# Table copies paced through a ScalarE cell, a third accumulator for the output projections, and two sums' buffers

## The chip, the cores and the metric

The kernel runs on one core of one Trainium2 chip. The metric is device time in microseconds (us): the median over runs. TensorE (PE) does matmuls, VectorE (DVE) and ScalarE (ACT) do elementwise work and empty the accumulators, GpSimd (POOL) does some elementwise work and issues a few transfers, SyncE (SP) issues most transfers. Each engine works through its own queue in order.

## What is computed

Two layers of a mixer network over T = 640 tokens (512 latent, 128 context) of width 2048. In float32 throughout, and cut to what matters here:

```python
mod = silu(cond) @ w_ada[l] + b_ada[l]            # 2048 x 6144, two condition vectors
shift, scale, gate = split(mod, 3)
h = rmsnorm(x, norm_g[l]) * (1 + scale) + shift
q, k, v, ag, lx, lg, hv, hx1, hx0, hg = split(h @ w_in[l])      # 2048 x 7168
att = diff_attention(q, k, v) * silu(ag)          # 8 heads
lru = rglru(conv(lx)) * silu(lg)
hy  = conv(hx0) * long_conv(conv(hv) * conv(hx1), hyena_filters) * silu(hg)
x = x + gate * (concat(att, lru, hy) @ w_out[l])  # 2048 x 2048
# after layer 2: y = rmsnorm(x, final_g); also context keys, values and LRU states
```

## The kernel before

**Projections.** Activations lie transposed as 16 chunks of 128 features by 640 tokens, each as a high and a low part (`A`). A weight block of 512 x 128 comes by one transfer (`wr`, line 380; four buffers). ScalarE casts it to `wh` and VectorE subtracts to `wl` (lines 177 and 178; four buffers each). `gemm` (line 418) computes one output chunk `m` from four such blocks, 24 matmuls of 320 columns each, into an accumulator `g` of two PSUM banks. The pool `pm` has two of these. Of the other four banks, two are the one buffer of `psS` (line 161), and two are the two buffers of `psT`, one bank each (line 164). The loads of a block are given a priority 600 places ahead of where they stand in the program. The framework makes each engine's queue from the program order, these priorities and its own planned times; a queue once made is run in order.

**Modulation steps.** `ada_steps` (line 327) is a generator, called `hook`. Each step loads one 128 x 512 piece of `w_ada` (`wa`, line 335) and makes two VectorE accumulations into `adas` (line 341). After 16 steps there is a seventeenth, "the turn": eight transposes into two `psT` (line 348) and two sums out of them (line 349). `adas` has one buffer. `gemm` advances the hook `hr` times per weight block, 1.5 in the output projection of layer 0, so six steps per chunk. Inside that projection (`wap` set) `wa` has four buffers.

**Tables.** After the second of the first three attention gates has been placed, `load_tabs` (line 746) allots the tables of the long convolution, in memory that the attention pool gives back. `tab_steps` (line 758) loads them in ten parts, one per weight block. So that a part is not fetched too early, GpSimd first copies one element of the block's `wh` into the part (line 762), then issues its transfer (line 763). The attention pool's last user is a transfer `rd<-oh` (line 1213). The third gate is the first product whose blocks pace the tables. The filters of the convolution (lines 593 to 640) come next in the program; their inputs are loaded by transfers on ScalarE's queue: `hid` (line 599), `w` (line 606), `drow` (line 622), `dec` (line 624). Line 632 multiplies into a `psT`, line 634 empties it.

**Output projection** (line 470). For chunk `m`, `old(m)` brings the residual. In layer 0 it is loaded as `xt`, transposed into the one `psS` (line 1268) and copied by ScalarE to `xo` (lines 1493 and 1494; two buffers). `new(m)` empties the accumulator with three VectorE instructions (line 1502) that read `xo`, then sums squares (lines 476 to 480). Chunks 0 and 1 are computed together; then `gemm` of chunk m stands ahead of `new(m)` in the program. Chunks 14 and 15 go through `gemm_parts` (line 396) together, in two halves of the tokens; the first three input projections of layer 1 go the same way, the third into `psS`. In layer 1 `turned` (line 1507) scales by `final_g`, transposes back into `psS` (line 1514) and copies to `Y` (lines 1518 and 1520). `stats` (line 461) uses a `psT`.

Of the kernel before, what the change touches and what calls it, by code (L numbers as in the profile page):

```python
# [20 lines left out]
NL = 512  # L21
# [115 lines left out]
class K:  # L137
# [189 lines left out]
    def ada_steps(self, todo):  # L327

        nc = self.nc
        for l, pc in todo:  # L330
            wv = self.i["w_ada"][l].rearrange("(a p) m -> p a m", p=128)
            acc = self.tl(self.sm, [128, 2, 512], tag="adas", bufs=1)
            for k in range(KC):
                w = self.tl(self.wap or self.W, [128, 512], F32, "wa", bufs=4 if self.wap else 2)
                nc.sync.dma_start(w, wv[:, k, pc * 512:(pc + 1) * 512])
                for s in range(2):
                    c = self.cs[:, k, s:s + 1]
                    if k == 0:
                        nc.vector.tensor_scalar(acc[:, s], w, c, None, op0=ALU.mult)
                    else:  # L340
                        nc.vector.scalar_tensor_tensor(acc[:, s], w, c, acc[:, s], op0=ALU.mult, op1=ALU.add)  # L341
                if k == KC - 1:
                    yield
                    sl = slice(pc * 4, pc * 4 + 4)
                    for s in range(2):
                        pt = self.psT()
                        for c in range(4):
                            nc.tensor.transpose(pt[:, c * 128:(c + 1) * 128], acc[:, s, c * 128:(c + 1) * 128], self.ident)
                        nc.vector.reduce_sum(self.par[l]["mod"][:, sl, s], pt.rearrange("p (c k) -> p c k", c=4), axis=AX.X)
                    self.ada_bias(l, pc * 4, 4)  # L350
                yield

    def ada_fin(self, l, c0, n, sb, tag):
# [41 lines left out]

    def gemm_parts(self, wd, ms, rhs, order, parts, keeps):

        nc = self.nc
        ps = [self.pm.tile([128, 2, 512], F32, name=self.nm("g_%d" % m), tag="m") if n < 2 else self.psS() for n, m in enumerate(ms)]
        ws = {}  # L400
# [16 lines left out]

    def gemm(self, wd, ms, rhs, order=range(KC)):

        nc = self.nc  # L420
        ps = [self.pm.tile([128, 2, 512], F32, name=self.nm("g_%d" % m), tag="m") for m in ms]
        for a in range(4):
            ks = order[4 * a:4 * a + 4]
            for m, p in zip(ms, ps):
                with self.tc.high_priority(offset=600):
                    wh, wl = self.load_w(wd, ks[0], m)
                self.last = wh
                if self.hook is not None:
# [317 lines left out]
    def load_tabs(self, pool):  # L746
# [4 lines left out]
        tp = self.tl(pool, [128, 2, 3, 128], F32R, tag="tp")  # L751
        self.tabs = (tb, rw, tp)
        w = 2 * TCE_W
        parts = [(tb[:, a, b, c:c + n], i["dft"][:, a, b, c:c + n]) for a in range(2) for b in range(2) for c, n in ((0, w), (w, 512))]
# [3 lines left out]
    def tab_steps(self, parts):  # L758
        nc = self.nc
        for t, src in parts:  # L760
            c = t if len(t.shape) == 2 else t[:, 0, 0, :]
            nc.gpsimd.tensor_copy(c[:, 0:1], self.last[:, 0, 0:1].bitcast(F32))
            nc.gpsimd.dma_start(t, src)
            yield True
# [705 lines left out]
    def out_proj(self, l):  # L1470
# [13 lines left out]
        def old(m):  # L1484
            xo = self.tl(pool, [128, T], tag="xo", bufs=2)
            if l == 0:
# [3 lines left out]
                nc.sync.dma_start(xt[:, 4, :], self.i["x_prompt"][0, :, c])  # L1490
                ps = self.psS()
                self.turn(lambda b: xt[:, b, :], 0, (ps[:, 0, :], ps[:, 1, :NP]))
                nc.scalar.copy(xo[:, :NL], ps[:, 0, :])
                nc.scalar.copy(xo[:, NL:], ps[:, 1, :NP])
            else:
# [11 lines left out]
        def turned(m, x, lo, hi):  # L1507

            V.tensor_scalar(x[:, lo:hi], x[:, lo:hi], self.par[l]["final_g"][:, m:m + 1], None, op0=ALU.mult)
            ps = self.psS()  # L1510
            b0, b1 = lo // 128, hi // 128
            for b in range(b0, b1):
                dst = ps[:, 0, b * 128:(b + 1) * 128] if b < 4 else ps[:, 1, :128]
                nc.tensor.transpose(dst, x[:, b * 128:(b + 1) * 128], self.ident)  # L1514
            c = slice(m * 128, (m + 1) * 128)
            bs = min(b1, 4)
            if b0 < bs:
                nc.scalar.copy(Y[:, b0:bs, c], ps[:, 0, b0 * 128:bs * 128].rearrange("p (b c) -> p b c", c=128))
            if b1 == 5:
                nc.scalar.copy(Y[:, 4, c], ps[:, 1, :128])  # L1520

# [14 lines left out]
        for m in range(KC - 2):  # L1536
# [3 lines left out]
            elif m > 1:  # L1540
                xos[m] = old(m)
                pq[m] = self.gemm(wd, [m * 128], ms, MIX_ORDER)[0]
            p = pq.pop(m)
# [11 lines left out]
        else:  # L1555
            parts = (0, HT, 0, 0), (HT, T, 1, 0)
        g = self.gemm_parts(wd, [m * 128 for m in zb], ms, MIX_ORDER, parts, [zp] * 8)
        p = dict(zip(zb, next(g)))
# [42 lines left out]
        first = [COL_HX0, COL_HG, COL_HX0 + 128]  # L1601
        g = self.gemm_parts(self.i["w_in"][1], first, hs, range(KC), ((0, HT, 0, 0), (HT, T, 1, 0)), [None] * 4 + [zp] * 8)
        ps = next(g)
# [51 lines left out]
```

## Time and profile before

| | |
|---|---|
| median of 3 runs | 2690.55 us (2690.27 to 2692.62) |
| the profiled execution's own time | 2696.49 us |
| its span, first to last instruction | 2694.7 us |
| mean granted TensorE clock | 0.984 |
| busy: PE, DVE, ACT, POOL | 96%, 71%, 40%, 10% |
| DMA over the span | 354.85 MB, mean 132 GB/s |

Times in rows are us from the span's start. In a timeline row stand start, duration, engine, line, operation, output <- inputs, shapes, how many instructions were merged, and in brackets the idle time of the engine before the first of them and what ended it. `SPq` and `ACTq` are issues of transfers. A granted clock of 1.00 is 2.4 GHz, 0.50 is 1.2 GHz.

### The profile page before, as it was taken

To read this page: it belongs to the slowest core of one execution; us is meant where nothing else is said; L and a number is where in the kernel's file an instruction comes from. 1 tells how busy PE (TensorE), PEld (TensorE's weight loads), DVE (VectorE), ACT (ScalarE), POOL (GpSimd) and SP (SyncE) were. 2 spreads that over 40 slices of the span, in tenths; PEclk is the share of its full clock that TensorE was granted. 3 is DMA by queue.
4 is the path that set the end of the run, shared out by engine and by line. 5 is a ranking of instruction groups with operands and counts; after the bars stand their busy time and mean duration, and the time that the engine had idled before them with its cause. 6 is when DMAs were issued, how large, how long until landed. Compare 5 with 4: busy or idle time off the path is not lost. (4 is left out here: it accounts for less than half of the span.)

```text
span 2694.7 us, 45940 instructions
## 1 busy us (share of the span) xinstructions
PE 2585.5 (96%) x17579; PEld 2491.2 (92%) x17579; DVE 1905.7 (71%) x3503; ACT 1074.9 (40%) x1965; POOL 280.1 (10%) x398
## 2 busy tenths in 40 slices
PE   6999999999999999989999999999999999999998
PEld 3689999999999999979988999999999989999997
DVE  5478779889888676578789467786887656565333
ACT  5224655454544222222234256545455522224222
POOL 2001210000001222100001022000000031120000
PEclk9999999999999999989999999999999999999999
DMA  9864233333333534577664422242332252345333
GB/s 283 295 192 134 80 104 106 101 95 118 97 115 111 170 112 137 163 238 228 206 201 136 126 73 82 87 118 68 104 90 63 59 157 87 112 143 169 91 99 116
DMA packets 442326, 354.85 MB, mean 132 GB/s; under 512 B 26401, under 2 KB 367216, under 8 KB 442106
## 3 DMA queue, kind: packets, MB, share of 16 engines
q1 hardware_dynamic: 428938, 336.39, 41.5%
q10 hardware_dynamic: 9280, 9.33, 1.1%
q0 software_dynamic: 3888, 6.20, 0.8%
q8 instruction: 138, 2.26, 0.4%
q14 instruction: 82, 0.67, 0.1%
HBM read 316.51 MB, written 35.32 MB: 131 GB/s over the span
## 5 line engine op out<-in xcount | busy, mean ns | idle before, releaser
L440 PE MATMUL g<-A,wh 128*128 128x320 f32 x8256 | 1595.3, 312 | 14.5 <-DVE xf L1502 9.4
L440 PEld LDWEIGHTS g<-A,wh 128*128 128x128 f32 x8256 | 1307.9, 189 | 17.8 <-issue 9.7
L440 PE MATMUL g<-A,wl 128*128 128x320 f32 x4128 | 953.8, 310 | 0.0
L177 ACT CAST wh<-wr 128x512 fp32r<-128x512 f32 x584 | 360.4, 619 | 972.3 <-PE g L440 664.3
L440 PEld LDWEIGHTS g<-A,wl 128*128 128x128 f32 x4128 | 695.5, 189 | 0.5 <-DVE wl L178 0.3
L178 DVE TENSOR_TENSOR wl<-wr,wh 128x512 fp32r<-128x512 f32 x584 | 421.5, 726 | 358.3 <-ACT wh L177 346.2
L341 DVE SCALAR_TENSOR_TENSOR adas<-wa,cs,adas 128x512 f32<-128x512 f32 x480 | 349.8, 763 | 31.7 <-DMA wa<-in_w_ada 30.1
L1233 ACT ACTIVATE e<-e,mx 128x768 f32<-128x768 f32 (+1 forms) x160 | 133.7, 836 | 67.0 <-DVE e L1232 66.6
L1232 DVE TENSOR_SCALAR_CACHE_REDUCE e<-pS 128x768 f32<-128x768 f32 (+1 forms) x160 | 131.3, 820 | 9.2 <-ACT e L1233 3.1
L1195 POOL TENSOR_TENSOR oq<-ot 128x640 f32<-128x640 f32 x16 | 20.9, 1303 | 898.0 <-ACT ot L1191 793.1
L732 PE MATMUL pS<-kk,qq 128*128 128x384 f32 (+1 forms) x288 | 100.9, 350 | 6.9 <-DVE e L1232 6.5
L540 PE MATMUL gp<-A,wh 128*128 128x320 f32 x512 | 103.9, 321 | 0.6 <-DVE e L546 0.3
L414 PE MATMUL g<-A,wh 128*128 128x320 f32 (+2 forms) x384 | 93.0, 326 | 10.9 <-ACT A L517 6.2
L540 PEld LDWEIGHTS gp<-A,wh 128*128 128x128 f32 x512 | 80.7, 191 | 18.3 <-issue 6.7
L732 PE MATMUL pS<-kl,qq 128*128 128x384 f32 (+1 forms) x288 | 96.0, 333 | 0.0
L178 DVE TENSOR_TENSOR wtl<-pt,wth 128x512 fp32r<-128x512 f32 (+1 forms) x144 | 70.4, 523 | 25.5 <-ACT wth L177 25.3
L177 ACT CAST wth<-pt 128x512 fp32r<-128x512 f32 (+1 forms) x144 | 59.7, 459 | 66.7 <-PE pt L1176 66.4
L414 PEld LDWEIGHTS g<-A,wh 128*128 128x128 f32 x384 | 67.7, 197 | 14.5 <-ACT A L517 7.2
L1502 DVE SCALAR_TENSOR_TENSOR xf<-g,mod,xo 128x128 f32<-128x128 f32 (+3 forms) x96 | 38.7, 436 | 55.4 <-PE g L440 20.4
L1239 DVE SCALAR_TENSOR_TENSOR e<-e,rz,e 128x768 f32<-128x768 f32 (+1 forms) x80 | 70.7, 883 | 1.7
L732 PEld LDWEIGHTS pS<-kk,qq 128*128 128x128 f32 x288 | 54.4, 189 | 17.5 <-DVE e L1232 12.2
L546 DVE TENSOR_TENSOR e<-e,gp 128x640 f32<-128x640 f32 x40 | 32.6, 818 | 41.5 <-PE gp L540 41.3
(376 smaller groups left out, 3258.2 us busy)
## 6 DMA issues: line engine op xcount, KB each, us to landing
wr<-in_w_in SPq DMA_DIRECT2D x448, 256.0 KB
wa<-in_w_ada SPq DMA_DIRECT2D x256, 256.0 KB
wr<-in_w_out SPq DMA_DIRECT2D x128, 256.0 KB
wada<-in_w_ada SPq DMA_DIRECT2D x28, 1024.0 KB
mx<-md SPq DMA_DIRECT2D x28, 320.0 KB
md<-ot SPq DMA_DIRECT2D x16, 320.0 KB
gm<-md SPq DMA_DIRECT2D x16, 320.0 KB
R<-rd SPq DMA_DIRECT2D x16, 320.0 KB
```

What stands on the lines that cost most here:

```text
L177: self.nc.scalar.copy(hi, src)
L178: self.nc.vector.tensor_tensor(lo, src, hi.bitcast(F32), op=ALU.subtract)
L341: nc.vector.scalar_tensor_tensor(acc[:, s], w, c, acc[:, s], op0=ALU.mult, op1=ALU.add)
L414: nc.tensor.matmul(p[:, j, o:o + c1 - c0], lhsT=w[:, c, :], rhs=rhs[k][x][:, c0:c1], start=(a == 0 and c == 0 and n == 0), stop=(a == 3 an ...
L440: nc.tensor.matmul(p[:, j, :HT], lhsT=w[:, c, :], rhs=rhs[k][x][:, j * HT:(j + 1) * HT], start=(a == 0 and c == 0 and n == 0), stop=(a == ...
L540: nc.tensor.matmul(p[:, j, :HT], lhsT=w, rhs=rhs[k0 + c][x][:, j * HT:(j + 1) * HT], start=(c == 0 and t == 0), stop=(c == n - 1 and t == 2))
L546: nc.vector.tensor_tensor(v, v, p[:, :, :HT], op=ALU.add)
L732: self.nc.tensor.matmul(out, lhsT=a, rhs=b, start=(n == 0), stop=(n == len(pairs) - 1))
L1232: V.tensor_scalar(e[:, :nk].rearrange("p (a b) -> p a b", a=nhf), ps[:, :nhf, :hw], -1.0, None, op0=ALU.mult, op1=ALU.min, accum_out=mx)
L1233: nc.scalar.activation(e[:, :nk], e[:, :nk], AF.Exp, scale=-1.0, bias=mx, accum_out=Z[:, c:c + 1])
L1239: V.scalar_tensor_tensor(es[0][:, :nk], es[1][:, :nk], rz[:, 1:2], es[0][:, :nk], op0=ALU.mult, op1=ALU.add)
L1502: V.scalar_tensor_tensor(x[:, a:b], p, mod[:, 32 + m, s:s + 1], xo[:, a:b], op0=ALU.mult, op1=ALU.add)
```

## The change

- The GpSimd copy of a table part reads a cell of a small tile `cells`; ScalarE writes that cell from the block's `wh`, once per weight block while tables are being loaded.
- In both output projections every third chunk (m = 2, 5, 8, 11, 14) accumulates in `psS`. `old` and `turned` use the two `psT` in place of `psS`.
- Inside the output projection of layer 0 `adas` gets two buffers of that pool's own, and the turn of one piece is made at the fourth step of the next. A piece takes 16 steps there, the last one 17.

```diff
     def ada_steps(self, todo):
         nc = self.nc
+        pend = None
         for l, pc in todo:
             wv = self.i["w_ada"][l].rearrange("(a p) m -> p a m", p=128)
-            acc = self.tl(self.sm, [128, 2, 512], tag="adas", bufs=1)
+            acc = self.tl(self.wap, [128, 2, 512], tag="adas", bufs=2) if self.wap else self.tl(self.sm, [128, 2, 512], tag="adas", bufs=1)
             for k in range(KC):
...
-                if k == KC - 1:
-                    yield
-                    sl = slice(pc * 4, pc * 4 + 4)
-                    for s in range(2):
...
-                    self.ada_bias(l, pc * 4, 4)
+                if k == 3 and pend is not None:
+                    self.ada_turn(*pend)
+                    pend = None
                 yield
+            pend = l, pc, acc
+            if not self.wap or (l, pc) == todo[-1]:
+                self.ada_turn(*pend)
+                pend = None
+                yield
+
+    def ada_turn(self, l, pc, acc):
+        nc = self.nc
+        for s in range(2):
+            pt = self.psT()
+            for c in range(4):
+                nc.tensor.transpose(pt[:, c * 128:(c + 1) * 128], acc[:, s, c * 128:(c + 1) * 128], self.ident)
+            nc.vector.reduce_sum(self.par[l]["mod"][:, pc * 4:pc * 4 + 4, s], pt.rearrange("p (c k) -> p c k", c=4), axis=AX.X)
+        self.ada_bias(l, pc * 4, 4)
 
-    def gemm_parts(self, wd, ms, rhs, order, parts, keeps):
+    def gemm_parts(self, wd, ms, rhs, order, parts, keeps, banks):
-        ps = [self.pm.tile([128, 2, 512], F32, name=self.nm("g_%d" % m), tag="m") if n < 2 else self.psS() for n, m in enumerate(ms)]
+        ps = [self.psS() if s else self.acc(m) for m, s in zip(ms, banks)]
 
-    def gemm(self, wd, ms, rhs, order=range(KC)):
+    def gemm(self, wd, ms, rhs, order=range(KC), third=False):
-        ps = [self.pm.tile([128, 2, 512], F32, name=self.nm("g_%d" % m), tag="m") for m in ms]
+        ps = [self.psS() if third else self.acc(m) for m in ms]
...
                     wh, wl = self.load_w(wd, ks[0], m)
-                self.last = wh
+                if self.tabl is not None:
+                    self.cn += 1
+                    nc.scalar.copy(self.cells[:, self.cn - 1:self.cn], wh[:, 0, 0:1].bitcast(F32))
...
     def load_tabs(self, pool):
+        self.cells, self.cn = self.tl(self.sm, [128, 16], tag="cell", bufs=1), 0
...
     def tab_steps(self, parts):
-            nc.gpsimd.tensor_copy(c[:, 0:1], self.last[:, 0, 0:1].bitcast(F32))
+            nc.gpsimd.tensor_copy(c[:, 0:1], self.cells[:, self.cn - 1:self.cn])
             nc.gpsimd.dma_start(t, src)
...
     def out_proj(self, l):
         def old(m):
-                ps = self.psS()
-                self.turn(lambda b: xt[:, b, :], 0, (ps[:, 0, :], ps[:, 1, :NP]))
-                nc.scalar.copy(xo[:, :NL], ps[:, 0, :])
-                nc.scalar.copy(xo[:, NL:], ps[:, 1, :NP])
+                pt, pp = self.psT(), self.psT()
+                self.turn(lambda b: xt[:, b, :], 0, (pt, pp[:, :NP]))
+                nc.scalar.copy(xo[:, :NL], pt)
+                nc.scalar.copy(xo[:, NL:], pp[:, :NP])
         def turned(m, x, lo, hi):
-            ps = self.psS()
...
+            for u, v in ((b0, min(b1, 4)), (max(b0, 4), b1)):
+                if u < v:
+                    pt = self.psT()[:, :(v - u) * 128]
+                    for b in range(u, v):
+                        nc.tensor.transpose(pt[:, (b - u) * 128:(b - u + 1) * 128], x[:, b * 128:(b + 1) * 128], self.ident)
+                    nc.scalar.copy(Y[:, u:v, c], pt.rearrange("p (b c) -> p b c", c=128))
...
-                pq[m] = self.gemm(wd, [m * 128], ms, MIX_ORDER)[0]
+                pq[m] = self.gemm(wd, [m * 128], ms, MIX_ORDER, m % 3 == 2)[0]
...
-        g = self.gemm_parts(wd, [m * 128 for m in zb], ms, MIX_ORDER, parts, [zp] * 8)
+        g = self.gemm_parts(wd, [m * 128 for m in zb], ms, MIX_ORDER, parts, [zp] * 8, (True, False))
...
-        g = self.gemm_parts(self.i["w_in"][1], first, hs, range(KC), ((0, HT, 0, 0), (HT, T, 1, 0)), [None] * 4 + [zp] * 8)
+        g = self.gemm_parts(self.i["w_in"][1], first, hs, range(KC), ((0, HT, 0, 0), (HT, T, 1, 0)), [None] * 4 + [zp] * 8, (False, False, True))
```

## Rows read from the trace of the kernel before

**Rows 1.** The page: span and busy time of each engine.

```profile
span 2694.7 us, 45940 instructions
PE 2585.5 (96%) x17579; PEld 2491.2 (92%) x17579; DVE 1905.7 (71%) x3503; ACT 1074.9 (40%) x1965; POOL 280.1 (10%) x398
```

**Rows 2.** Waits of PE over the span: us in total, times, longest.

```profile
PE g L440 <- DVE xf L1502: 9.4, 1, 9.4
...
PE pt L632 <- DVE sx L634: 5.5, 1, 5.5
PE pt L632 <- DMA w<-in_hy_w: 4.4, 1, 4.4
PE g L440 <- ACT wh L177: 4.1, 2, 3.6
...
PE g L414 <- DVE xf L1502: 2.9, 2, 1.9
```

**Rows 3.** Stretches after PE's waits: engines' busy us (instructions), granted clock, DMA share, GB/s.

```profile
870.00:876.40 6.40, 6.40 (x23) 6.13 (x24) 6.40 (x10) 1.66 (x3) 6.30 (x13) 0.50 0.84 211
...
1185.10:1190.40 5.30, 5.28 (x20) 5.30 (x21) 5.30 (x10) 1.92 (x4) 0.00 (x0) 0.50 0.84 266
...
1371.30:1374.70 3.40, 3.40 (x13) 3.40 (x14) 3.40 (x6) 1.38 (x3) 0.00 (x0) 0.51 0.72 235
...
891.00:896.90 5.90, 5.88 (x20) 5.54 (x21) 4.58 (x7) 0.62 (x1) 4.64 (x5) 0.50 0.62 188
...
2200.10:2204.20 4.10, 4.06 (x13) 3.50 (x14) 0.69 (x1) 0.00 (x0) 0.25 (x1) 0.58 1.21 344
```

**Rows 4.** The output projection of layer 0 in stretches, columns as in rows 3.

```profile
1175.00:1190.00 15.00, 5.55 (x23) 5.33 (x23) 14.92 (x29) 2.01 (x4) 0.00 (x0) 0.56 0.86 260
1190.00:1360.00 170.00, 170.00 (x1181) 169.88 (x1181) 137.30 (x241) 47.76 (x84) 0.00 (x0) 1.00 0.73 221
```

**Rows 5.** Timelines of SP, POOL and ACT where layer 0 loads its tables.

```profile
866.41 0.54 SPq L1213 DMA_DIRECT2D rd<-oh  x1
868.54 1.62 POOL L762 CAST tb<-wh 128x1 fp32r<-128x1 f32 x4 [29.01 <-DMA rd<-oh]
869.30 0.62 ACT L177 CAST wh<-wr 128x512 fp32r<-128x512 f32 x1 [2.18 <-POOL tb L762]
```

**Rows 6.** Timeline of ACT and its transfers where layer 1 loads its tables.

```profile
2187.37 2.18 ACT L177 CAST wh<-wr 128x512 fp32r<-128x512 f32 x4 [10.79 <-POOL tb L762]
...
2192.79 1.13 ACTq L606 DMA_DIRECT2D w<-in_hy_w  x2
```

**Rows 7.** Timelines of ACT and DVE where layer 0's filters begin.

```profile
880.84 0.62 ACT L177 CAST wh<-wr 128x512 fp32r<-128x512 f32 x1 [8.98 <-DMA wr<-in_w_in]
...
884.09 2.18 ACTq L624 DMA_DIRECT2D dec<-in_decay  x3
...
888.26 1.42 DVE L341 SCALAR_TENSOR_TENSOR adas<-wa,cs,adas 128x512 f32<-128x512 f32 x2 [6.08 <-DMA wa<-in_w_ada]
```

**Rows 8.** Timelines of PE, DVE and ACT as layer 0's output projection begins.

```profile
1174.44 1.23 PE L348 MATMUL pt<-ident,adas 128*128 128x128 f32 x8
...
1177.68 6.71 DVE L341 SCALAR_TENSOR_TENSOR adas<-wa,cs,adas 128x512 f32<-128x512 f32 x10
1184.30 1.72 DVE L1502 SCALAR_TENSOR_TENSOR xf<-g,mod,xo 128x192 f32<-128x192 f32 x5
...
1185.65 0.57 ACT L1493 COPY xo<-pS 128x512 f32<-128x512 f32 x1
```

**Rows 9.** DVE by line, 1160 to 1390: busy us, mean ns, idle before.

```profile
L178 DVE TENSOR_TENSOR wl<-wr,wh 128x512 fp32r<-128x512 f32 x61 | 42.0, 691 | 27.1 <-ACT wh L177 18.9 <-PE pt L348 7.7 <-DMA xt<-in_x_sample 0.3
...
L349 DVE TENSOR_REDUCE mod<-pt 128x4 f32<-128x512 f32 x12 | 7.8, 683 | 3.2 <-PE pt L348 3.1
```

**Rows 10.** Timelines of ACT and PE in the tail: a small copy, the last statistics.

```profile
2674.24 0.20 ACT L454 ACTIVATE st<-st 128x3 f32<-128x3 f32 x1
...
2684.05 0.27 ACT L1518 COPY Y<-pS 128x128 f32<-128x128 f32 x1 [0.34 <-PE pS L1514]
...
2684.22 0.61 PE L467 MATMUL pt<-onesr,acc 128*128 128x2 f32 x4 [0.20 <-DVE acc L480]
```

More of the change, by code (lines that the diff above doesn't have):

```diff
@@ L341, in ada_steps @@
                         nc.vector.scalar_tensor_tensor(acc[:, s], w, c, acc[:, s], op0=ALU.mult, op1=ALU.add)
-                if k == KC - 1:
-                    yield
-                    sl = slice(pc * 4, pc * 4 + 4)
-                    for s in range(2):
[L346 to L349, printed above, removed]
-                    self.ada_bias(l, pc * 4, 4)
-                yield
+                if k == 3 and pend is not None:
+                    self.ada_turn(*pend)
+                    pend = None
+                yield
+            pend = l, pc, acc
[11 more added lines that the diff above has]
+        self.ada_bias(l, pc * 4, 4)
     def ada_fin(self, l, c0, n, sb, tag):
@@ L416, in gemm_parts, with acc @@
                 yield
-    def gemm(self, wd, ms, rhs, order=range(KC)):
+    def acc(self, m):
+        return self.pm.tile([128, 2, 512], F32, name=self.nm("g_%d" % m), tag="m")
+    def gemm(self, wd, ms, rhs, order=range(KC), third=False):
         nc = self.nc
-        ps = [self.pm.tile([128, 2, 512], F32, name=self.nm("g_%d" % m), tag="m") for m in ms]
+        ps = [self.psS() if third else self.acc(m) for m in ms]
         for a in range(4):
@@ L1509, in turned @@
             V.tensor_scalar(x[:, lo:hi], x[:, lo:hi], self.par[l]["final_g"][:, m:m + 1], None, op0=ALU.mult)
-            ps = self.psS()
+            c = slice(m * 128, (m + 1) * 128)
             b0, b1 = lo // 128, hi // 128
[L1512 to L1520, printed above, removed]
+            for u, v in ((b0, min(b1, 4)), (max(b0, 4), b1)):
[4 more added lines that the diff above has]
+                    nc.scalar.copy(Y[:, u:v, c], pt.rearrange("p (b c) -> p b c", c=128))
         def store(r, b0):
```

## The prediction

> **What bounds the kernel now.** The page comes first: PE is busy for 2585.5 of 2694.7 us [rows 1], so at most 109 us are idle on it, and a change that leaves the matmuls alone can win only idle time, or time at the lower clock. The second view is PE's waits. Five of its groups touch what is edited: 9.4 us in one piece for an accumulator that VectorE has not emptied, 1.9 us for another, 3.6 and about 0.5 us for a `wh` block, and 5.5 and 4.4 us for the filters [rows 2]. The third view is the granted clock just after these waits: 0.50 to 0.58 where it is 1.00 in the long undisturbed stretch, that is 1.2 instead of 2.4 GHz for all or nearly all of the stretch, each time after PE had stood still [rows 3, 4]. So a wait costs more than its idle time. How much more comes from the same rows: the undisturbed stretch has 1181 matmuls in 170 us, 6.95 per us [rows 4]. In 870.0 to 876.4 there are 23 matmuls, worth 3.3 us at that rate, so 3.1 us are lost; in 1185.1 to 1190.4 20 matmuls, 2.4 us lost; in 1371.3 to 1374.7 13 matmuls, 1.5 us lost [rows 3]. A few records can be missing, which would make these losses smaller.
>
> **Tables, layer 0.** The copy on POOL waits for memory of the attention pool, which the transfer issued at 866.41 frees; it runs at 868.54. Until then it holds the `wh` blocks that it is to read, ScalarE's next cast waits for it (2.18 us, released at 869.30), and PE waits 3.6 us for the cast [rows 2, 5]. With the cell, ScalarE reads its own block and POOL holds only a cell, so the cast waits for PE alone. Removed: 3.6 + 3.1 = 6.7 us. Added: one copy of one column per block, eleven per layer, 22 in all. The nearest row is a three-column ScalarE instruction of 0.20 us [rows 10], so 4.4 us on an engine that is busy 40% of the span [rows 1]; hidden, and if all of it were exposed it would cost those 4.4 us. POOL's own copy and transfers are unchanged in number. Behind POOL's wait stand only its memsets for the filters, which wait as they do now.
>
> **Tables, layer 1.** The same wait holds four casts until 2187.37 [rows 6], but PE loses only about 4.1 - 3.6 = 0.5 us [rows 2]. Removed: 0.5 us.
>
> **Start of layer 0's output projection.** Chunks 0 and 1 fill both accumulators. PE makes a turn at 1174.44 and then needs chunk 0's accumulator for chunk 2. VectorE runs ten modulation accumulations first, 6.71 us, and empties the rest of chunk 0 from 1184.30 [rows 8]. With `psS` as a third accumulator, chunk 2 needs nothing of VectorE; its 96 matmuls take 96/6.95 = 13.8 us [rows 4], while chunks 0 and 1 are emptied by about 1186. Removed: 9.45 us idle, written 9.4 [rows 2], and 2.4 us of low clock, 11.8 us. VectorE does not get the pause in which it now catches up, and stays some 10 us behind. With three accumulators a chunk may be emptied up to two chunks late, 27 us, so this is covered; and VectorE works 137.3 of the 170 us after it [rows 4]. Part of its idle time there is PE's turn, 7.7 + 3.1 us of it [rows 9], which two buffers for the sums and the later turn should shorten.
>
> **End of layer 0's output projection.** Chunk 15 now needs chunk 13's accumulator, just computed. In the ring it takes chunk 12's. Removed: 1.9 + 1.5 = 3.4 us.
>
> **What lies beside other work.** `old` and `turned` move from `psS` to `psT` with the same number of transposes and copies, so at nothing as long as a `psT` is free. The copies of `old` also wait for an `xo`, which chunk m - 2 must have left: the one at 1185.65 came only after that [rows 8]. So `old` can hold both `psT` for some 10 us, and turns need the same two. There are six turns in this stretch (12 sums [rows 9]). I take 2.0 us for all such waits; the bounds are 0 and six waits of the size of layer 0's table stall, 40 us (that end is the third rival). In layer 1's tail the last statistics (2684.22) would need a `psT` that a copy begun at 2684.05 frees after 0.27 us [rows 10]: 0.1 us later, up to 0.7 if the next copies come first; taken as 0.1. The five steps fewer only end the modulation work earlier. All are small beside the waits.
>
> **The filters behind the tables** are not edited, but their waits hang on the same queues. In layer 0 ScalarE's cast at 880.84 had waited 8.98 us for a weight load and the loads of `dec` went out only at 884.09, behind it; VectorE was held by `wa` until 888.26 [rows 7]. In layer 1 `w` went out at 2192.79, behind the casts that POOL held [rows 6]. Weights loaded before the rush of table transfers would free these. Gone altogether, they give back 5.5 + 3.0 us (20 matmuls in 5.9 us) and 4.4 + 2.2 us (13 in 4.1 us) [rows 2, 3], 15.1 us. On the other side, POOL's transfers begin at the same time as before while PE arrives up to 6.7 + 0.5 us earlier, so up to 7.2 us of what was won may be waited out here. I take 0, between both ends, since rows speak for either.
>
> **Sum.** 6.7 + 0.5 + 11.8 + 3.4 = 22.4 us removed, 2.1 us given back: -20.3 us. The profiled execution took 2696.5 us, 5.9 above the median shown; it becomes 2676.2, and the median 2690.55 becomes **2670.3 us**. What a measurement here can tell from no change is about 0.2%, 5.4 us.
>
> **Rivals.**
> First, the ring only defers. If VectorE and the transfers cannot make up what PE's pause now gives them, PE meets an unfinished accumulator some chunks later and the 11.8 us come back: 2682.1. For it: in 1175 to 1190 VectorE is busy 14.92 of 15 us and the transfers run at 260 GB/s. Against it: 221 GB/s and 81% of VectorE in the 170 us that follow [rows 4]. The Trainium skill has a case that speaks for this rival: TensorE: Matmul & The Clock Gate, section HAM oscillation — how this bites in real kernels, reports that for a thin matmul "Adding PSUM double-buffering gave no further gain". By it the two terms of the ring would be 0; the trace disagrees as far as it goes, since one of the waits is for an accumulator and nothing else.
>
> Second, the tables' stall moves to the filters, by the 7.2 us above: 2677.5. For it: layer 1 has little table stall and yet 4.4 us at the filters [rows 2]. Against it: what is late there is late because of the casts.
>
> Third, **slower**: the two `psT` become the bottleneck of layer 0's output projection. Place: a turn's transposes stand in PE's queue behind an `old` whose copies wait for `xo`. Price: 6.7 us each with its low clock, as at the tables; six turns, 40 us, in place of the 2.0 us taken: 2670.3 - 2.0 + 40 = 2708.3. It turns the sum from a gain to a loss when a turn waits 22.3/6 = 3.7 us on average. For it: both users share two buffers and the copies do wait. Against it: the sums of a turn are ready four steps earlier than it is issued, and after the start chunk m - 2 is long empty when `old(m)` copies.
>
> Fourth, it does not do what it says: the queues are made anew, and POOL, the cast or the third accumulator stays tied to the old event, for instance because ScalarE's copy is put behind something late. Then all of it is within a few us of 2690.
>
> **How the numbers follow.** Forecast (all four stalls gone) 0.61, first rival 0.13, second 0.12, third 0.08, fourth 0.06. The forecast's own unknowns run from -15.1 to +7.2 us at the filters and some us at `psT`: 2655 to 2680. The range reaches on to the first rival and a little above, 2657 to 2686, and leaves out the third and fourth rivals and the last bit at the low end. Faster: forecast, first and second rival less 0.04 for a spill into the band, 0.82. Same: fourth rival and that spill, 0.10. Slower: the third, 0.08.
>
> **What would show it.** Right: near 866 ScalarE's casts wait for PE, not for POOL, and PE has no 3.6 us wait; after the turn near 1174 PE goes on with matmuls into `pS` at a granted clock of 1.00; no wait for `xf` before line 414 at the end of that projection. Wrong: PE waiting before line 1268 or 348 for copies or sums; a wait for `xf` before chunk 3, 4 or 5; a longer wait before line 632. A clock that falls at new places would say that other waits took over.

## The result and the profile after

The kernel after takes 2665.96 us (median of 5 runs, 2661.26 to 2669.93) where the kernel before, beside it, took 2691.83: a ratio of 0.9906, 95% interval 0.9895 to 0.9917. That is 25.9 us faster; 20.3 had been forecast, and 2670.3 us lies 4.3 us above what was measured. The profiled execution of after is its slowest, 2669.93 us.

The page of the kernel after, against [rows 1]; PE's busy time is 9.1 us less for the same 17579 matmuls, at a mean granted clock of 0.991 instead of 0.984.

```profile
span 2668.2 us, 45971 instructions
PE 2576.4 (97%) x17579; PEld 2482.0 (93%) x17579; DVE 1903.2 (71%) x3503; ACT 1077.8 (40%) x1987; POOL 276.2 (10%) x398
```

Waits of PE over the whole span of after (us in total, times, longest), against [rows 2]. The 9.4 us for `xf` and the 3.6 us for `wh` are gone. The wait at the filters (line 632 before, 646 now) is not, and two waits for ScalarE's copies to `xo` and one for `gout` are new. Layer 1's first products waited 6.2 us for ScalarE's normalised chunks `A` before (first fence) and wait 1.6 us now (second fence):

```profile
PE g L414 <- ACT A L517: 6.2, 4, 3.8
```

```profile
PE pt L646 <- DVE sx L648: 6.0, 2, 5.1
PE pt L358 <- ACT xo L1508: 4.1, 1, 4.1
...
PE pt L746 <- DVE gout L627: 3.1, 1, 3.1
...
PE g L423 <- ACT A L531: 1.6, 1, 1.6
PE pt L1283 <- ACT xo L1508: 1.6, 1, 1.6
```

Engines' busy us, granted clock, DMA share and GB/s of after in stretches, columns as in [rows 3, 4]. The first two lines are the place of the old table stall, at full clock now; the third and fourth follow PE's waits for `sx` and for `gout` and still show 1.2 GHz; 1175 to 1190 has 102 matmuls where before had 23; in the 170 us after it VectorE is busy 161.17 us, up from 137.30, and PE no longer all the time; the last line is a new dip.

```profile
866.00:870.00 4.00, 4.00 (x29) 4.00 (x28) 3.34 (x6) 2.25 (x4) 1.87 (x6) 1.00 0.74 221
870.00:876.40 6.40, 6.38 (x40) 5.94 (x39) 3.90 (x7) 0.62 (x1) 6.36 (x17) 1.00 1.20 280
882.30:885.70 3.40, 2.85 (x8) 2.52 (x9) 2.23 (x4) 0.81 (x2) 2.93 (x8) 0.51 1.04 340
909.60:913.00 3.40, 3.00 (x12) 3.00 (x13) 1.95 (x4) 1.33 (x4) 0.00 (x0) 0.50 0.70 206
...
1175.00:1190.00 15.00, 14.50 (x102) 14.19 (x101) 14.83 (x28) 4.83 (x10) 0.00 (x0) 1.00 0.81 254
1190.00:1360.00 170.00, 164.56 (x1142) 163.54 (x1140) 161.17 (x280) 48.19 (x87) 0.00 (x0) 1.00 0.81 248
1360.10:1363.50 3.40, 3.26 (x14) 3.26 (x15) 2.78 (x6) 0.26 (x2) 0.00 (x0) 0.50 0.60 187
```

**Where the time went.** ScalarE casts the same 584 weight blocks in the same order in every kernel here. The start of the n-th cast in one trace, less that in the trace of before, is how far that kernel is ahead at that point. The table gives the change of this lead over each stretch (us, minus is won), for all kernels of this study. In the trace of before the stretches begin and end at: tables of layer 0, 839.6 to 937.7; the stretch behind them, to 1158.7; start of the output projection, to 1191.0; its middle, to 1361.0; its end, to 1395.7; norms and layer 1's first products, to 1467.1; tables of layer 1, 2161.7 to 2232.7. What lies outside is left out (in after -1.2 ahead of the tables, -0.1 between, +0.8 behind).

| kernel | tables 0 | behind | start | middle | end | norms | tables 1 |
|---|---|---|---|---|---|---|---|
| after | -3.0 | -0.6 | -12.4 | +2.8 | +2.4 | -9.3 | -5.9 |
| e1 cell alone | -3.8 | -2.7 | +0.2 | +0.1 | +0.1 | +0.4 | -6.4 |
| e2 ring alone | -0.2 | 0.0 | -13.2 | +0.2 | -2.6 | -1.6 | -0.3 |
| e3 sums alone | -2.0 | -3.0 | +1.7 | +2.5 | +0.2 | -9.4 | +0.9 |
| e23 ring and sums | -0.2 | -1.3 | -10.3 | +3.3 | +3.0 | -8.7 | -0.4 |
| e4 own buffer, turn at once | -3.1 | +0.9 | -12.8 | +7.9 | -1.4 | -9.0 | -6.1 |
| e5 third xo | -4.0 | -1.7 | -11.3 | +1.5 | +1.4 | -9.3 | -6.2 |
| e6 steps moved | -4.3 | -5.0 | -13.1 | +2.1 | +2.3 | -9.2 | -6.7 |
| e7 no steps in gates | -0.5 | -1.3 | -0.7 | -0.7 | -0.5 | +0.8 | +1.4 |
| e8 piece late, old sums | -3.4 | -1.5 | -13.0 | +1.2 | -2.5 | -10.0 | -6.1 |
| e9 piece late, new sums | -2.9 | -1.2 | -10.6 | +0.1 | -3.0 | -9.1 | -6.0 |
| e10 no tables in layer 0 | -5.7 | -2.0 | -11.8 | +3.3 | +2.5 | -9.0 | -7.1 |
| e11 tables paced slower | -3.6 | -3.1 | -12.3 | +3.7 | +1.8 | -9.3 | -7.2 |

Each row is one execution. Stretches of unchanged code give the noise: tables of layer 1 +1.4 to -0.4 in the four kernels without the cell, tables of layer 0 -0.2 to -2.0 in the same four, and the 840 us ahead of the tables, left out above, +0.1 to -5.2 over all kernels. Short falls of the clock come and go between executions (last section), so differences of 1 to 2 us in one stretch carry nothing.

The casts run ahead of PE, so a slip of the casts need not be one of PE. The same lead taken from PE's own 13824 matmuls on `wh` and `wl` shows where PE loses: from 1200 to 1361 of before it moves by 1.0 us at most in every kernel (after -16.0 to -15.6, e2 -17.1 to -16.6, e4 -18.6 to -18.1), whatever stands under "middle". All that PE loses in the projection it loses behind 1361, at its last chunks. From 1200 to 1395.7 that is, on PE: after +4.0, e2 -2.5, e23 +5.6, e4 +6.5, e5 +2.3, e8 -1.3, e9 -3.4. So "middle" and "end" are read together here.

### The profile page after: what moved, and what is told of

Read it like the earlier page. It is cut to its first block, busy times and chain, and to the rows that moved or that the text cites. A ratio compares the mean times of both kernels' runs of the same rounds, so it can differ in the third digit from the quotient of the medians.

```text
span 2668.2 us, 45971 instructions
## 1 busy us (share of the span) xinstructions
PE 2576.4 (97%) x17579; PEld 2482.0 (93%) x17579; DVE 1903.2 (71%) x3503; ACT 1077.8 (40%) x1987; POOL 276.2 (10%) x398
## 3 DMA queue, kind: packets, MB, share of 16 engines
q8 instruction: 138, 2.26, 0.3%
## 4 chain that ended last, share of the span: by engine, by line
PE 74%; DVE 12%; DMA 7%; issue 3%; ACT 2%; POOL 1%; SPq 0%; ACTq 0%; DVEq 0%; POOLq 0%
PE g L454 49%; PE pS L746 6%; PE pt L746 5%; DVE adas L342 4%; PE gp L554 4%; PE pS L454 3%; DMA wa<-in_w_ada 3%; DVE wl L178 2%; PE g L423 2%; PE pt L1191 2%; PE pS L423 1%; PE pa L319 1%; ACT wh L177 1%; DMA yy<-gd 1%; DMA mx<-md 1%
## 5 line engine op out<-in xcount | busy, mean ns | idle before, releaser
L454 PE MATMUL g<-A,wh 128*128 128x320 f32 x7744 | 1497.5, 312 | 1.1 <-DVE A L178 1.1
L454 PEld LDWEIGHTS g<-A,wh 128*128 128x128 f32 x7744 | 1223.5, 189 | 3.0 <-DVE A L178 1.6
L454 PE MATMUL g<-A,wl 128*128 128x320 f32 x3872 | 895.4, 310 | 0.0
L454 PEld LDWEIGHTS g<-A,wl 128*128 128x128 f32 x3872 | 650.7, 188 | 0.0
L454 PE MATMUL pS<-A,wh 128*128 128x320 f32 x512 | 96.7, 310 | 0.0
L454 PEld LDWEIGHTS pS<-A,wh 128*128 128x128 f32 x512 | 80.2, 188 | 0.0
L423 PE MATMUL g<-A,wh 128*128 128x320 f32 (+2 forms) x256 | 60.6, 322 | 3.9 <-ACT A L531 1.6
```

The lines of the kernel that those rows point to most:

```text
L423: nc.tensor.matmul(p[:, j, o:o + c1 - c0], lhsT=w[:, c, :], rhs=rhs[k][x][:, c0:c1], start=(a == 0 and c == 0 and n == 0), stop=(a == 3 an ...
L454: nc.tensor.matmul(p[:, j, :HT], lhsT=w[:, c, :], rhs=rhs[k][x][:, j * HT:(j + 1) * HT], start=(a == 0 and c == 0 and n == 0), stop=(a == ...
```

## The experiments

All were timed in five rounds beside the kernel before. The ratio comes from all runs and differs a little from that of the two medians.

| run | median us | before beside it | ratio, 95% interval |
|---|---|---|---|
| e1 | 2683.94 | 2693.65 | 0.9966, 0.9955 to 0.9978 |
| e2 | 2676.84 | 2693.65 | 0.9947, 0.9932 to 0.9961 |
| e3 | 2687.44 | 2693.65 | 0.9983, 0.9972 to 0.9994 |
| e23 | 2677.85 | 2693.65 | 0.9947, 0.9934 to 0.9960 |
| e4 | 2666.35 | 2691.01 | 0.9902, 0.9888 to 0.9916 |
| e5 | 2667.10 | 2691.01 | 0.9906, 0.9890 to 0.9921 |
| e6 | 2664.49 | 2691.01 | 0.9898, 0.9882 to 0.9914 |
| e7 | 2690.14 | 2691.01 | 0.9994, 0.9985 to 1.0004 |
| e8 | 2660.12 | 2689.82 | 0.9888, 0.9867 to 0.9909 |
| e9 | 2666.19 | 2689.82 | 0.9914, 0.9898 to 0.9930 |
| e10 | 2665.74 | 2691.42 | 0.9901, 0.9888 to 0.9915 |
| e11 | 2666.93 | 2689.82 | 0.9917, 0.9902 to 0.9931 |

**e1: the cell alone**, on the kernel before.

```diff
-                self.last = wh
+                if self.tabl is not None:
+                    self.cn += 1
+                    nc.scalar.copy(self.cells[:, self.cn - 1:self.cn], wh[:, 0, 0:1].bitcast(F32))
...
-            nc.gpsimd.tensor_copy(c[:, 0:1], self.last[:, 0, 0:1].bitcast(F32))
+            nc.gpsimd.tensor_copy(c[:, 0:1], self.cells[:, self.cn - 1:self.cn])
```

> The kernel before with the tables' cell alone. The main theory (three parts that act in separate places) expects what the comparison of the two traces shows in the two stretches of tables and filters: about -3 us in layer 0 and about -6 us in layer 1, so about -9 us, 2682 to 2684 us against 2691.8; the wait of 3.6 us for a wh block near 866 gone, the 9.4 us wait at the start of layer 0's output projection still there. The rival, that the tables' stall only moves to the filters and that the -6 us of layer 1 are a consequence of the output projection being earlier, expects under 3 us, 2689 us or more.

As expected: 1 - 0.9966 of 2693.65 is 9.2 us, -3.8 and -6.4 in the two stretches of tables. The stall of layer 0's output projection stands (9.3 us); so what is won in layer 1 does not come from the projection.

**e2: the ring alone**, modulation sums as before; beside this line, the parts of the change for `old`, `turned` and `gemm_parts`.

```diff
-                pq[m] = self.gemm(wd, [m * 128], ms, MIX_ORDER)[0]
+                pq[m] = self.gemm(wd, [m * 128], ms, MIX_ORDER, m % 3 == 2)[0]
...
```

> The kernel before with the ring of three accumulators alone (old's and turned's transposes in psT), modulation sums as before. The main theory expects the 9.4 us wait and its low clock gone, -11.8 us, and at the end of that projection about 0 to -3 us: 2677 to 2681 us. If the deferred turn is what makes room for psT, turns and old collide here: more waits of 2 to 6 us before the turn's transposes and a time of 2683 or more. The rival that the ring only defers expects 2690.

14.3 us (1 - 0.9947 of 2693.65). Nothing is deferred: the middle stays at +0.2, the end wins 2.6. The norms keep their 6.2 us for `A` (first line). PE's waits of e2 from 1150 to 1460 hold one of 0.3 us at a turn and none for `xo`, so the two `psT` suffice for `old` and the turns:

```profile
PE g L414 <- ACT A L520: 6.2, 3, 4.0
PE pt L1271 <- DMA xt<-in_x_sample: 3.3, 2, 2.5
PE g L414 <- DVE xf L1505: 1.0, 1, 1.0
PE g L414 <- DVE A L523: 0.6, 2, 0.4
PE pt L348 <- DVE adas L341: 0.3, 1, 0.3
```

**e3: the new `ada_steps` alone; e23: ring and new `ada_steps`** (the parts of the change as they are in its diff).

> The kernel before with the two sums' buffers and the later turn alone, two accumulators as before. The main theory holds the 10 us that were won between the end of layer 0's output projection and layer 1's first products to come from this part (the last turn earlier, the next generator's sums out of the way of the norms): 2680 to 2684 us, with the 9.4 us wait still there in whole or most. The rival, that they come from PE's earlier arrival by the ring, expects 2689 to 2693.

> The kernel after without the cell: ring and sums together. If the parts add, this is after plus what the tables' part is worth, 2673 to 2676 us (after: 2666.0). If ring and sums need each other, it is lower than the sum of the two single parts by over 3 us; if they take the same idle time, higher by over 3 us.

e3 wins the 9.4 us at the norms without any ring, so they do come from the sums' part; but its whole gain is 4.6 us (by the interval 1.6 to 7.5), between the two expectations. Its trace has the projection slower by 1.7 + 2.5 us. With the ring (e23) no gain of the part is to be told: 0.9947 with it and without it. It wins 7 us at the norms (-8.7 against -1.6) and loses 3 at the start and 8.7 over middle and end. What the part wins at the norms it gives back in the projection; the expected 2673 to 2676 was wrong.

**e4: sums in one buffer of the projection's own pool, turn at once.** On the kernel after.

```diff
-            acc = self.tl(self.wap, [128, 2, 512], tag="adas", bufs=2) if self.wap else self.tl(self.sm, [128, 2, 512], tag="adas", bufs=1)
+            acc = self.tl(self.wap or self.sm, [128, 2, 512], tag="adas", bufs=1)
...
```

> The kernel after, but each turn comes right after its sums as before, and the sums have one buffer of the out-projection's pool instead of two. The theory after the four single parts: the ring's own gain at the end of that projection (-2.6 us with the ring alone, +3.0 with ring and sums) is eaten by the later turn, and the 10 us before layer 1's first products come from the sums' own memory alone. Then here: no wait of 4 us before the last turn's transposes, no slip of 3 us during the projection, the 10 us kept; 2658 to 2662 us against 2666 of after. The rival, that two buffers and the later turn are what wins the 10 us, expects 2672 to 2677.

The first half held: the 9.0 us at the norms need neither a second buffer nor the later turn. The second half fell: without the later turn middle and end together lose 6.5 us (on PE also 6.5), with it 5.2 (on PE 4.0). So the turn's place is not what makes the projection late. What e4 shares with after, and e2 does not, is that `adas` of the pool `sm` lies free during the projection. The next to ask for it is the first piece of layer 1's next four (columns 8), which stands behind the whole projection in the program. With one shared buffer it must wait for the last turn, and its sums stand between the norms; with the buffer free, the framework can put them among the projection's last chunks. That it is this piece is shown by e8 and e9 below, which move it alone.

The trace shows it in the sums' own busy time. VectorE is the third pair of numbers (busy us and instructions on `adas`), stretches 1190 to 1360, 1360 to 1385 and 1385 to 1450. The kernel before:

```profile
1190.00:1360.00 170.00, 4.14 (x32) 3.72 (x32) 83.54 (x124) 0.00 (x0) 1.00 0.73 221
1360.00:1385.00 25.00, 1.04 (x8) 0.94 (x8) 14.72 (x22) 0.00 (x0) 0.93 0.55 170
1385.00:1450.00 65.00, 1.82 (x8) 1.40 (x8) 22.06 (x30) 0.00 (x0) 0.92 0.59 178
```

The kernel after:

```profile
1190.00:1360.00 170.00, 4.39 (x32) 3.64 (x32) 107.77 (x159) 0.00 (x0) 1.00 0.81 248
1360.00:1385.00 25.00, 1.97 (x8) 1.57 (x8) 11.82 (x17) 0.00 (x0) 0.93 0.53 160
1385.00:1450.00 65.00, 1.25 (x8) 0.89 (x8) 6.78 (x10) 0.00 (x0) 0.97 0.47 139
```

Thirty instructions stood among the norms and ten do now; 124 in the projection have become 159. Part of these 35 comes from PE's earlier start (e2 has 139 instructions and 94.07 us, and e8 below, with that piece kept out, 138 and 92.74 us); the other 21, 15 us, are the piece, and VectorE's emptying of accumulators stands in one queue with them.

**e5: a third `xo`.** On the kernel after.

```diff
-            xo = self.tl(pool, [128, T], tag="xo", bufs=2)
+            xo = self.tl(pool, [128, T], tag="xo", bufs=2 if last else 3)
```

> The kernel after with a third xo buffer in layer 0's output projection. If the waits of 4.05 and 1.63 us for ScalarE's copies come from the copies waiting for an xo (that is the third rival's mechanism), both go with the dip at 1360: 5 to 7 us less than after, 2659 to 2661. If the two psT themselves are short, or VectorE is simply late, the waits stay: 2665 to 2667.

The first of the two is right about the wait and wrong about the time. PE's waits for `xo` shrink from 4.1 and 1.6 us to one of 0.5, and an accumulator that VectorE has not emptied stops PE instead. PE's waits of e5, 1150 to 1460:

```profile
PE pS L423 <- DVE xf L1517: 3.4, 1, 3.4
...
PE pt L1283 <- ACT xo L1508: 0.5, 1, 0.5
```

From the start of the projection to the end of its last chunks e5 is 1.2 us better than after (-8.4 against -7.2), which is not to be seen in the time. On PE from 1200 to 1395.7 e5 loses 2.3 us where after loses 4.0. VectorE is late, and the place at which PE meets that is secondary.

**e7: no modulation steps in layer 1's first gates.** On the kernel before.

```diff
-RATE = (dict(lru=.25, att=.75, ag1=.75, hv=.75, ag2=0, out=1.5), dict(gate=.5, lru=.5, att=.5, ag1=.5, hv=.5, ag2=0, out=0))
+RATE = (dict(lru=.25, att=.75, ag1=.75, hv=.75, ag2=0, out=1.5), dict(gate=0, lru=.5, att=.5, ag1=.5, hv=.5, ag2=0, out=0))
```

> The kernel before with no modulation steps during layer 1's first gates. If the 10 us between the end of layer 0's output projection and layer 1's first products are lost to the next generator's sums that share VectorE and the loading queue with the norms, this alone brings most of them: 2682 to 2685 against 2692 to 2694. If they hang on when the projection ends, or on the memory of the sums as such, nothing: 2690 to 2694.

No change, but the test did not do what it should: 26 sums still stand on VectorE from 1385 to 1450 (30 in before). A later place in the program alone does not move them. That the framework brings them forward as soon as their buffer is free fits this and was not looked into. The run says nothing on the cause. Sums of e7, that stretch:

```profile
1385.00:1450.00 65.00, 1.82 (x8) 1.40 (x8) 19.02 (x26) 0.00 (x0) 0.89 0.57 171
```

**e8 and e9: the piece kept out by its memory.** Its sums get memory of a pool that is free only after the norms. e8 has the cell, the ring and the old `ada_steps` (below, against the kernel before); e9 is the kernel after with the same choice in its second branch.

```diff
-            acc = self.tl(self.sm, [128, 2, 512], tag="adas", bufs=1)
+            acc = self.tl(self.lrup if (l, pc) == (1, 8) else self.sm, [128, 2, 512], tag="adas", bufs=1)
```

> Cell and ring as in the kernel after, the sums and turns as before (one buffer, turn at once), and the sums of the piece that follows the output projection (columns 8 of layer 1) put into memory of the lru pool, which is free only after the norms. The theory now: what the sums' part of the change does is to free the old buffer, so that VectorE takes that piece during the output projection; this costs some 8 us there (slips and the wait near 1360) and wins 10 us between the norms and layer 1's first products. With the piece kept out of both: the ring's whole gain (start and end, about -16) and the 10 us, so about 2657 to 2661 against 2666 of after. The rival, that two buffers and the later turn are themselves of use, expects 2666 or more.

> The kernel after, with that same piece in the lru pool, two buffers and the later turn kept. If the piece taken early is what makes VectorE late in the output projection, the slip of 3 us there and the wait of 4 us near 1360 go: 2657 to 2661, as with the single buffer. If the later turn itself brings the collisions in psT, the wait of 4 us stays and this is 3 to 6 us above the one with the single buffer.

e8 came out as expected, 2660.12 us. With the piece in neither place, the norms' stretch still wins 10.0 us, against 1.6 in e2, which leaves the piece in its old place; and the projection's end wins 2.5 where after lost 2.4. VectorE's busy time in the projection falls to 148.21 of 170 us and PE is at work for 168.75 (after: 164.56). The windows of e8, all instructions and then the sums alone:

```profile
1190.00:1360.00 170.00, 168.75 (x1170) 167.75 (x1170) 148.21 (x259) 49.28 (x87) 0.00 (x0) 1.00 0.77 237
...
1385.00:1450.00 65.00, 0.00 (x0) 0.00 (x0) 8.26 (x12) 0.00 (x0) 1.00 0.40 117
```

e9 shows the same in its trace (middle +0.1, end -3.0, no wait near 1360) and is 6.3 us ahead of after at the end of the two profiles; but its profile is of its fastest run and that of after of its slowest, and its median, 2666.19, is that of after. So the trace confirms the mechanism in e9 and the times do not; what separates e9 from e8, 6.1 us by the medians, stays open, since that wait is in neither. e8 is 5.8 us below after by the medians, and the fastest of all kernels here; the two ratios' intervals overlap (0.9867 to 0.9909 and 0.9895 to 0.9917), so that it beats after is likely and not shown.

**e6, e11 and e10: what holds layer 0's filters.** All on the kernel after. e6 takes the modulation steps out of the table stretch (rate 0, half as many again later); e11 paces the first four parts at every second block and puts them in the order of need; e10 fills layer 0's tables with zeros in place of the ten transfers, so it leaves out what the filters compute from them. Shown are the lines on which each rests.

```diff
+            self.hr = 0
             for h in range(2, NAG):
...
-                self.hr = rate["hv"]
...
                 for j in range(4):
+                    self.hr = rate["hv"] * 1.5 * (j > 0)
```

```diff
             nc.gpsimd.dma_start(t, src)
             yield True
+            if n < 4:
+                yield True
...
```

```diff
+            if l == 0:
+                nc.gpsimd.memset(t.bitcast(F32), 0.0)
+            else:
+                nc.gpsimd.dma_start(t, src)
```

> The kernel after, with no modulation steps in layer 0 while the tables load (none for the last gate before them and for the first of four turns of the hyena projections; the other three have half as many again, so the same total). If the wait of 5.10 us at the filters is held by VectorE's wait for wa, it goes with its dip, 4 to 7 us: 2659 to 2662. If it is held by the loads of dec behind the tables' transfers, 2664 to 2667 and the wait is still there, now with VectorE waiting for dec itself.

> The kernel after, with the first four parts of the tables paced at every second weight block instead of every one, and those that are needed first put first. If the wait of 5.1 us at layer 0's filters is held by the burst of table transfers (five parts start together near 868), it falls under 2 us, and with it the issue of dec of 7.2 us: 4 to 7 us less than after, 2659 to 2662. If it is held by something else, 2665 to 2668; if the tables come too late, a wait for tb or rw shows and it is slower.

> The kernel after with layer 0's tables filled with zeros by POOL instead of loaded, so that layer 0's hyena filters are computed from zeros; ten transfers of 2.7 MB in all are left out, the cells and POOL's copies stay. If the tables' transfers are what holds the filters (by the loads they crowd out), the wait of 5.1 us near 882 and the 2.0 us beside it fall under 1.5 us together and the dip of the clock goes: 6 to 10 us less up to weight block 188, about 2657 to 2660 in all. If VectorE's and ScalarE's other loads are late without the tables as well, the wait stays at 4 us or more and the time within 2 us of after.

First the kernel after: timelines of ACT with its transfers, DVE and POOL near 880. Two loads of `dec` take 7.20 us to go out, ScalarE stands behind them, VectorE waits for `wa` until 881.35, and only then comes the product that PE needs. The five waiting copies on POOL run together, and five transfers follow at once.

```profile
873.12 7.20 ACTq L638 DMA_DIRECT2D dec<-in_decay  x2
880.37 0.28 ACT L441 COPY cell<-wh 128x1 f32<-128x1 f32 x2 [6.65 <-DMA dec<-in_decay]
...
881.35 0.75 DVE L342 SCALAR_TENSOR_TENSOR adas<-wa,cs,adas 128x512 f32<-128x512 f32 x1 [3.93 <-DMA wa<-in_w_ada]
882.02 0.68 DVE L648 TENSOR_TENSOR sx<-pt,dec 128x512 f32<-128x512 f32 x1
...
868.07 1.69 POOL L777 CAST tb<-cell 128x1 fp32r<-128x1 f32 x5 [29.73 <-DMA hid<-hd]
869.82 0.95 POOL L619 MEMSET w<- 64x1024 f32 x1
870.72 2.74 POOL L778 DMA_DIRECT2D tb<-in_dft  x5
```

e6 failed like e7: VectorE still does modulation sums there and waits 3.85 us for `wa` at the same place (DVE of e6). PE's wait is 4.8 us and the time that of after.

```profile
877.44 0.75 DVE L342 SCALAR_TENSOR_TENSOR adas<-wa,cs,adas 128x512 f32<-128x512 f32 x1 [3.85 <-DMA wa<-in_w_ada]
```

e11 starts three parts together instead of five, and the wait stays at 4.5 us. e10 has no table transfers at all: PE's wait falls to 2.4 us and that dip of the clock goes, while 3.2 us for `gout` stay and 1.2 us for `sl` stand where after has 0.3. (The 2.0 us of the expectation lie some 70 us later, at 951.09, and stand at that place in before, after and e10 alike.) The stretch wins 2.7 us more than in after. The time, 2665.74 us, is that of after. ACT of e10:

```profile
872.25 4.22 ACTq L638 DMA_DIRECT2D dec<-in_decay  x2
876.51 0.28 ACT L441 COPY cell<-wh 128x1 f32<-128x1 f32 x2 [3.66 <-DMA md<-gm]
```

So the tables' transfers hold about half of that wait. That they do it by crowding the other loads (280 GB/s from 870 to 876.4 in after, 340 from 882.3) is likely and not shown by itself. The rest is there without them: the two loads of `dec` still take 4.22 us to go out, and the trace names the store of the last gate (`md`) as what ended ScalarE's wait behind them. A kernel without that dependence was not run; this part stays open.

## Why the prediction was right, and where it was not

The sum, -20.3 us, was near to -25.9, and the sign and main term were right; but several terms were wrong, and they cancelled in part: that the sum came so near is partly luck. Forecast and measured, in us: tables of layer 0 -6.7 and -3.0; the projection as a whole -13.2 (-11.8 - 3.4 + 2.0) and -7.2; norms 0 and -9.3; tables of layer 1 -0.5 and -5.9. The fourth rival, that nothing happens, falls with e1 and e2, each clear of 1.

- **Start of the output projection, -11.8.** Measured -12.4 in after and -10.3 to -13.2 wherever the ring is. In the old place PE now goes on into `pS` at a granted clock of 1.00. The first rival falls with e2, where neither the casts nor PE lose anything in the middle. The case cited with it from the Trainium skill (TensorE: Matmul & The Clock Gate, section HAM oscillation — how this bites in real kernels) does not carry over: by it the ring would give 0, and e2 measures a ratio of 0.9947. The reason given beforehand, that the wait here was for an accumulator alone, fits; the skill's kernel was not run here.
- **End of the projection, -3.4.** Right for the ring by itself (e2 -2.6, e8 -2.5, e9 -3.0), wrong for the whole change (+2.4).
- **2.0 us for `psT`, and the third rival.** Its mechanism came once, and with it one of the signs that the prediction had named as wrong: a turn's transposes waited 4.05 us at 1360.24, behind an `old` whose copies were late, with a dip after it. At 1353.38 the transposes of an `old` itself waited 1.63 us. Twice in one projection, not at each of six turns, and far from the 3.7 us on average that would have decided. The step that failed is "VectorE works 137.3 of the 170 us after it", taken as the cover for the ring: the ring alone brings VectorE to 149.52 of these 170 us (e2, first line below) without either wait, and the piece that the change lets in brings it to 161.17 (against e8's 148.21). Nor is the share by itself what decides, since PE loses nothing up to 1361 of before; it is what stands in front of one emptying. PE, DVE and ACT of after at that place, below the line of e2: VectorE stands 1.97 us for a `wa`, makes four sums, and empties chunk 13 only from 1357.76, which frees its `xo`; ScalarE stands 5.49 us for that with the squares of line 493, then copies at 1359.62; the turn can start. Whether the load or the sums weigh more here was not separated.

```profile
1190.00:1360.00 170.00, 169.95 (x1179) 168.93 (x1178) 149.52 (x260) 49.18 (x87) 0.00 (x0) 1.00 0.77 238
```

```profile
1353.38 0.77 PE L1283 MATMUL pt<-ident,xt 128*128 128x128 f32 x5 [1.63 <-ACT xo L1508]
...
1360.24 1.97 PE L358 MATMUL pt<-ident,adas 128*128 128x128 f32 x8 [4.05 <-ACT xo L1508]
...
1354.50 2.74 DVE L342 SCALAR_TENSOR_TENSOR adas<-wa,cs,adas 128x512 f32<-128x512 f32 x4 [1.97 <-DMA wa<-in_w_ada]
...
1357.76 1.12 DVE L1517 SCALAR_TENSOR_TENSOR xf<-g,mod,xo 128x320 f32<-128x320 f32 x3
...
1358.98 0.74 ACT L493 ACTIVATE sq<-xf 128x640 f32<-128x640 f32 x1 [5.49 <-DVE xf L1517]
1359.62 0.57 ACT L1508 COPY xo<-pt 128x512 f32<-128x512 f32 x1
1360.09 0.27 ACT L1509 COPY xo<-pt 128x128 f32<-128x128 f32 x1
```

- **The five steps fewer "only end the modulation work earlier".** This sentence failed outright, and hid the largest unforeseen term: -9.3 us at the norms. Freeing the shared buffer moved another generator's sums across the projection. The prediction counted the buffers that the change adds, not the one that it gives back. On balance no gain of that part can be told with the ring (e23 against e2), which is one reason why the forecast sum stayed close.
- **Tables, layer 0, -6.7.** ScalarE's wait for POOL and PE's 3.6 us are gone as said, and the clock of that stretch is 1.00 where it was 0.50 [rows 3]; but by the end of the stretch only 2.9 to 4.3 us are left in the kernels with the cell and the tables (e3, without the cell, has 2.0 there, so the noise is not small beside that). PE comes earlier to filters that are not ready earlier: 5.1 us at 882.85 where it was 5.5, and 3.1 us more at line 746. That is the second rival's mechanism, at about half of its price of 7.2.
- **Tables, layer 1, -0.5, and the filters at 0.** Measured -5.9 to -7.2 in every kernel with the cell. This is the bound that was written down and not taken: 4.4 + 2.2 us for the late `w` of layer 1. ScalarE's casts no longer wait for POOL, so its loads of `w` go out at 2166.60 and 2169.46, and PE, which comes to their products at 2172.33 and 2173.93, does not wait for them. Before, they went out from 2192.79 [rows 6], 3.0 us before PE came to the first product, and PE waited 4.37 us. What is left is 0.94 us for `sx` at the third product. (The raw times do not compare: after is 21.4 us ahead here anyway.) One zero for both layers was the mistake: in layer 1 ScalarE's own stall held the loads, in layer 0 the tables' transfers and something that stays open do. PE of before, then ACT and PE of after, layer 1:

```profile
2200.14 3.12 PE L632 MATMUL pt<-w,hid 128*128 128x256 f32 x8 [4.37 <-DMA w<-in_hy_w]
```

```profile
2166.60 0.48 ACTq L620 DMA_DIRECT2D w<-in_hy_w  x1
...
2169.46 0.47 ACTq L620 DMA_DIRECT2D w<-in_hy_w  x1
...
2179.41 1.10 PE L646 MATMUL pt<-w,hid 128*128 128x256 f32 x4 [0.94 <-DVE sx L648]
```

- **The added copies at nothing.** Right: 0.19 us each, and e1 shows no loss beyond 0.4 us in any stretch of the table. The tail's 0.1 us cannot be told apart: from the tables of layer 1 to the last instruction after loses 0.8 us, e1, with the old tail, 2.0.

## What to carry to other kernels

When a change gives a tile buffers of its own, ask who was waiting for the old buffer: the framework may move that work forward, as here, into the stretch whose slack the change relies on. To move work, tie it to memory or data that is free at the right time, as e8 and e9 do; two experiments here that only changed its place in the program (e6, e7) did not clear the place they were meant to clear. And where one stall holds an engine that also issues loads, price the loads behind it layer by layer: what they wait for may differ.

## What was not expected of the hardware

The prediction charged a low clock to every long wait. The same wait in the same code brings it in one execution and not in another. Near 684 PE waits 2.23 us in e9 and 2.26 us in after for ScalarE's `qs`; behind it the granted clock is 0.50 for 3.3 us in e9 and 1.00 in after. PE of e9, and its window (13 matmuls):

```profile
684.43 0.90 PE L1172 MATMUL pt<-ident,qs 128*128 128x128 f32 x3 [2.23 <-ACT qs L1166]
...
684.30:687.60 3.30, 3.17 (x13) 3.18 (x14) 3.30 (x7) 1.87 (x5) 0.00 (x0) 0.50 0.57 166
```

PE of after, and its window (20 matmuls):

```profile
685.61 0.66 PE L1172 MATMUL pt<-ident,qs 128*128 128x128 f32 x4 [2.26 <-ACT qs L1166]
...
685.50:688.80 3.30, 3.13 (x20) 2.87 (x21) 3.30 (x8) 1.90 (x6) 0.00 (x0) 1.00 0.57 162
```

Seven matmuls fewer in equal time are 1.0 us at the 6.95 per us of the prediction. That such dips make up the spread between executions is likely and not shown; the spread is there: executions of e10 lie up to 9.5 us apart (2659.41 to 2668.91), those of the kernel before beside e4 to e7 14.5 us (2683.80 to 2698.30). So two single profiles that differ by a third of a per cent tell nothing by their ends, while a stretch whose value repeats over many kernels does.
